# Turning more attention weights by VectorE and DRAM, normalising in the gate, one shared stretch of SBUF, and a planner with backward passes

## The chip, the cores and the metric

The kernel runs on one core of one Trainium2 chip. The metric is the device time of one execution in microseconds (us). A measurement runs the kernel several times and takes the median; a profiled execution gives the trace from which all rows come. Engines are named as the profile names them: PE (TensorE matmul), PEld (TensorE weight load), DVE (VectorE), ACT (ScalarE), POOL (GpSimd) and SP (SyncE, which here issues every DMA).

## The reference

One layer of a hybrid encoder on 1024 prompt rows and 32 sample rows of width 1024, all in float32:

```python
hn = rmsnorm(h, g_pre)
qa, ka, va, ga, qb, kb, vb, gb = split(hn @ w_in)      # 8 x 512 columns, 8 heads of 64 each side
# A: band attention with a clipped relative bias; a frame sees its chunk of 64 and 8 chunks before it
sA = qa @ ka.T * 64 ** -0.5 + bias[rel]
oa = softmax(where(band, sA, -1e30)) @ va
# B: stick-breaking attention, strictly causal
z = qb @ kb.T * 64 ** -0.5
log_1m = where(causal, log_sigmoid(-z), 0)
ob = where(causal, exp(log_sigmoid(z) + reverse_cumsum(log_1m) - log_1m), 0) @ vb
y = concat(oa * silu(ga), ob * silu(gb)) @ w_out
h = h + rmsnorm(y, g_post)
h = h + sigmoid(h @ w_ple_gate) * (p @ w_ple)
```

The keys and values are outputs too. The sample rows attend to a cache of 512 rows as well.

## The kernel before, in words

**Precision.** Every float32 product is done with operands split into a high part and a remainder (`...h` and `...l`, type fp32r), in two or three matmuls.

**Recording and planning.** The body does not emit instructions. A `Recorder` stores each operation with its operands; all get the line of one helper in the profile (L515), so tiles must be told apart by name. `order()` then walks through a model of the engines, with a planner's cost for each operation (`cost`), a start and a margin for each DMA (`DMA_START`, `DMA_MARGIN`), and picks for each engine the ready operation of the lowest key. A key is the place at which the operation was recorded, shifted by the hand-kept tables `AHEAD_OF` and `AHEAD_AT`. The result is a fixed order on every queue. DMAs all stand in SP's queue.

**Stages.** First come norms, transposes of `x` (`ptx`) and a part of the product with `w_ple` (`ple`). Then eight attention stages, pairs of heads in the order A0, B0, A1, B1, ... A3, B3. Each pair p has two heads. While a pair's attention runs, `weave` mixes in the projections of the next pair (`col_steps`, tiles `mm_kA` and so on, 72 matmuls of 352 columns for each output of 128 columns), so that PE has other work between the steps of attention. The last stage holds the gate projections `gA`, `gB` instead. Last come the output products (`o0P` to `o3P`) and the gate products (`g0P` to `g3P`).

**One head of attention** is `attention(ab, p, h)`. It goes over eight query tiles i of 128 rows. `scores(i)` multiplies the queries `L` with `kd` and `kl` into PSUM (`SA`, `SB`). For A, DVE adds the bias and takes the running minimum of the negated scores into `om`, ACT takes the exponential into `be` with the row sum in `statA`, DVE takes the reciprocal and POOL scales `be` by it. For B two sigmoids, a scan and a product on POOL do the same job. A's tile i sees the blocks i-4 to i, so tiles 4 to 7 have five blocks of 128 keys.

`weights_t(i)` turns the weights, keys onto partitions, and splits them into `wTh` (ACT) and `wTl` (DVE). It does this in one of two ways. Either PE transposes each 128x128 block into PSUM (`ptwA`, `ptwB`), four blocks to a bank. Or, for the tiles in `ROUND`, DVE transposes 32x32 squares (`om<-be`), one DMA writes the result to DRAM (`swapA`, `swapB`), and four DMAs read it back in place (`be<-swapA`). `ROUND` names tile 5 for A and tiles 4, 5 and 6 for B.

`values(g)` multiplies the turned weights of four query tiles with the values into `PVA` or `PVB`; g is 0 for tiles 0 to 3 and 1 for tiles 4 to 7. For g = 1 of A, its first matmul reads a block that all four tiles see, so it needs tile 7's weights at once. Tiles are turned `LAG_T` = 2 units behind their scores, and values follow behind that.

**Buffers.** The attention weights lie in two rings, `Arena` "om" (3076 columns) and "be" (3640), which are granted in recording order; turned weights lie in two more rings.

**The gate** (`mms` in `col_steps`, kind "g") loads the head pair's output `og` from `o_dr`, computes acc * sigmoid(acc) and multiplies it by `og` on POOL.

Of the kernel before, what the change touches and what calls it, by code (L numbers as in the profile page):

```python
# [13 lines left out]
P = 128  # L14
# [14 lines left out]
    ('ACT', 'L'): 329, ('ACT', 'S'): -1196, ('ACT', 'be'): -16, ('ACT', 'kd'): 796,  # L29
    ('ACT', 'newh'): -56, ('ACT', 'oT'): -600, ('ACT', 'om'): -36, ('ACT', 'p'): -23,  # L30
    ('ACT', 'v'): 51, ('DVE', 'Kl'): 1140, ('DVE', 'Vh'): -16, ('DVE', 'gT'): -158,
    ('DVE', 'om'): -178, ('DVE', 'ot'): 166, ('DVE', 'uu'): -34, ('DVE', 'vt'): 131,
    ('DVE', 'wl'): 758, ('DVE', 'wls'): 131, ('POOL', 'kl'): 934, ('POOL', 'wl'): 27,
    ('SP', 'GP'): 272, ('SP', 'Kcs'): -461, ('SP', 'be'): 17, ('SP', 'o'): 49,
    ('SP', 'pp'): -611, ('SP', 'stv'): -823,
}
AHEAD_AT = {
    (0, 'ACT', 'sq'): -249, (0, 'DVE', 'pleo'): -309, (1, 'ACT', 'stv'): 1111, (1, 'DVE', 'stat'): -309,
    (1, 'PE', 'ptw'): 174, (2, 'ACT', 'be'): 54, (2, 'ACT', 'v'): 127, (2, 'ACT', 'wTh'): -885,
    (2, 'ACT', 'wh'): -57, (2, 'DVE', 'S'): -238, (2, 'DVE', 'ot'): -112, (2, 'DVE', 'vx'): -293,  # L40
    (3, 'ACT', 'Kh'): -162, (3, 'ACT', 'be'): 443, (3, 'ACT', 'ot'): -574, (3, 'ACT', 'stq'): 399,
    (3, 'ACT', 'w'): 692, (3, 'ACT', 'wTh'): -1352, (3, 'DVE', 'Kcs'): -84, (3, 'DVE', 'S'): -1167,
    (3, 'DVE', 'Vh'): 222, (3, 'DVE', 'w'): -332, (3, 'PE', 'PV'): 1076, (3, 'PE', 'Ss'): 1432,
    (3, 'SP', 'kd'): -118, (3, 'SP', 'kl'): -63, (4, 'ACT', 'be'): 76, (4, 'ACT', 'om'): 38,
    (4, 'DVE', 'S'): -1067, (4, 'DVE', 'vt'): -1007, (4, 'DVE', 'wTl'): 571, (5, 'ACT', 'stq'): -509,
    (5, 'ACT', 'wh'): 1431, (5, 'DVE', 'stat'): 886, (5, 'DVE', 'vt'): -279, (5, 'POOL', 'om'): -449,
    (6, 'ACT', 'be'): 27, (6, 'ACT', 'v'): 29, (6, 'ACT', 'wTh'): 103, (6, 'DVE', 'om'): 123,
    (6, 'DVE', 'ot'): 37, (6, 'POOL', 'ksS'): 600, (6, 'POOL', 'om'): 364, (6, 'SP', 'be'): 463,
    (7, 'ACT', 'newh'): 1036, (7, 'ACT', 'wTh'): -428, (7, 'DVE', 'L'): -198, (7, 'DVE', 'S'): 1202,
    (7, 'DVE', 'Vl'): -1133, (7, 'DVE', 'kt'): 76, (7, 'DVE', 'om'): 204, (7, 'DVE', 'w'): -825,  # L50
    (7, 'DVE', 'wTl'): -310, (7, 'PE', 'ptw'): 1440, (7, 'SP', 'bias'): -214, (7, 'SP', 'o'): 69,
    (7, 'SP', 'swap'): -328, (8, 'ACT', 'sgg'): -941, (8, 'DVE', 'S'): -79, (8, 'DVE', 'Vl'): 272,
    (8, 'DVE', 'om'): 183, (8, 'DVE', 'sgg'): -911, (8, 'POOL', 'sgg'): 256, (8, 'SP', 'Kcs'): 610,
# [8 lines left out]
ROUND = {"A": ((5,),), "B": ((4,), (5,), (6,))}  # L62
LAG_T = 2
LAG_V = 2
SPACE_S = {'A': 0.15, 'B': 0.05}
SPACE_T = {'A': 0.35, 'B': 0.4}
SPACE_V = {'A': 0, 'B': 0}
PARTS = 4
BEHIND = 2
RATES = (1.0, 0.84, 0.92, 0.94, 1.0, 0.88, 1.14, 1.0)  # L70
# [135 lines left out]
class Op:  # L206
    __slots__ = ("pieces", "eng", "what", "args", "kw", "key", "busy", "late", "ready", "left", "after", "at", "size", "shared", "table")
# [9 lines left out]
DVE_SET, POOL_SET = 137, 110  # L217


class Pool:  # L220
# [8 lines left out]
    def tile(self, shape, dtype, tag=None, name=None, bufs=1):  # L229
        b = Buf(shape, dtype, self, tag or name, name, bufs)  # L230
        line = self.tags.setdefault(b.tag, [])
        b.room = b.tag if bufs == 1 else f"{b.tag}.{len(line) % bufs}"
        after = {line[-1].place} if line else {self.opened} if self.opened else set()
        b.place = self.rec.node("CTL", b.take, (), {}, after)
        if len(line) >= bufs:
            self.rec.turns.append((b.place, line[len(line) - bufs]))
        self.ops.append(b.place)
        line.append(b)
        return b
# [47 lines left out]

class Engine:
# [9 lines left out]
class Recorder:  # L298


    def __init__(self):
        self.with_table, self.old_table, self.stage = [], [], 0
# [32 lines left out]
    def node(self, eng, what, args, kw, after):  # L335
# [3 lines left out]
        o.shared, o.table = False, None  # L339
# [3 lines left out]
    def add(self, eng, what, args, kw):  # L343
# [31 lines left out]
        n = o.key[2]  # L375
        o.key = o.key[0], n + AHEAD_OF.get(kind, 0) + AHEAD_AT.get((self.stage, *kind), 0), n
# [17 lines left out]
    def cost(eng, method, args, kw, writes, reads):  # L394
# [18 lines left out]
        if eng == "POOL":  # L413
            if method == "tensor_tensor":
                if n == 1:
                    return 400, 0
                return 200 + (1.9 if out.buf.dtype == F32 else 2.3) * n, 0
# [10 lines left out]
    def order(self):  # L428

        import heapq  # L430
        for place, old in self.turns:
            place.after.update(x[0] for x in old.uses)
        users = {id(o): [] for o in self.ops}
        for o in self.ops:
            o.left, o.ready = len(o.after), 0.0
            for a in o.after:
                users[id(a)].append(o)
# [3 lines left out]
        now = {e: [] for e in names}  # L441
        for o in self.ops:
            if not o.left:
                heapq.heappush(soon[o.eng], (0.0, o.key, id(o), o))
        out, port, line, table, away, flying = [], 0.0, 0.0, AF.Exp, [], 0
        while len(out) < len(self.ops):
# [11 lines left out]
            while soon[e] and soon[e][0][0] <= t:  # L458
                _, key, n, o = heapq.heappop(soon[e])
                heapq.heappush(now[e], (key, n, o))  # L460
            o = heapq.heappop(now[e])[2]
            if o.shared and e == "DVE" and port > t + DVE_SET:
                held = [x for x in now[e] if not x[2].shared]
                if held:
                    heapq.heappush(now[e], (o.key, id(o), o))
# [3 lines left out]
                    o = pick[2]  # L469
            o.at = t  # L470
            if e == "CTL":
                done = t
            elif e == "SP":
# [4 lines left out]
                o.at = t  # L478
# [5 lines left out]
            else:  # L484
# [6 lines left out]
                done = t + o.busy + o.late  # L491
            out.append(o)
            for u in users[id(o)]:
# [4 lines left out]
                u.ready = max(u.ready, r)  # L498
                u.left -= 1
                if not u.left:  # L500
                    heapq.heappush(soon[u.eng], (u.ready, u.key, id(u), u))
        return out

# [17 lines left out]
def stream_step(  # L521
# [26 lines left out]
    r_dr = scratch([8, 768], "r_dr")  # L548
    vs_dr = {ab: scratch([4, P, NS], f"vs_dr{ab}") for ab in "AB"}
    ple_dr = scratch([T, D], "ple_dr")  # L550

# [27 lines left out]
    ring0, ring1 = Arena(rec, at, "om", 3076), Arena(rec, at, "be", 3640)  # L579
# [50 lines left out]
    def load_x(t):  # L630
# [3 lines left out]
        xt = x34[0][:, (t - 3) * D:(t - 2) * D] if 3 <= t < 7 else ring0.tile([P, D], f"x{t}")  # L634
# [9 lines left out]
    def scale_x(t, xt, n, gp):  # L644
        sq = ring1.tile([P, D], f"sq{t}")
# [44 lines left out]
    def bias_rows():  # L690

        rb = ring0.tile([8, 257], "rb")
        dma(rb, rel_bias[0])
        nc.vector.tensor_scalar(rb, rb, -1.0, None, ALU.mult)
        R = ring1.tile([8, 768], "R")
# [49 lines left out]
    def prep_v(nm, h, tok):  # L745
        r, o = halves(h)
        v2 = opnd[h].tile([P, 8, P], F32R, tag=f"v2{h}", name=f"v2{nm}{h}")
        nc.scalar.copy(v2[:, :, r], tok[:, 0:8, r])
        nc.vector.tensor_tensor(v2[:, :, o], tok[:, 0:8, r], f(v2[:, :, r]), ALU.subtract)
# [17 lines left out]
    def keys_out(ab, p, src, o_p, o_s):  # L767
# [4 lines left out]
        def turn():  # L772
            out = at2.tile([P, NT, P], F32, tag="tok", name=f"kt{ab}{p}", bufs=2)
            x = out.rearrange("p b c -> p (b c)")[:, 0:n + NS]
# [9 lines left out]
    def values_out(ab, p, src, o_p, o_s, then):  # L784
# [5 lines left out]
        def turn():  # L790
# [8 lines left out]
            out = at2.tile([P, NT, P], F32, tag="tok", name=f"vt{ab}{p}", bufs=2)  # L799
            box["out"] = out  # L800
            nc.vector.transpose(out[:, 8, 0:NS], st[:, SEQ:T])

        def back():
            out = box["out"]
            nc.scalar.copy(out[:, 0:8, :].rearrange("p b (g f) -> p g b f", g=4), src()[:, 0:SEQ].rearrange("p (g b f) -> p g b f", g=4, f=32))
            later(o_p[0, 0, :, h2, :].rearrange("(b p) h d -> p b (h d)", p=P), out[:, b0:8, :])
            sample_rows(o_s[0, 0, :, h2, :].rearrange("p h d -> p (h d)"), out[:, 8, 0:NS])
            then(out)
# [9 lines left out]
    def col_steps(j):  # L818
# [53 lines left out]
        def after_v(tok):  # L872
            src_of["v", ab, p] = tok
            dma(vs_dr[ab][p], tok[:, 8, 0:NS])
# [11 lines left out]
    def attention(ab, p, h):  # L886
# [22 lines left out]
        def rooms(i):  # L909
# [3 lines left out]
            if g not in whole:  # L913
                n = sum(cost(x) for x in g) * P
                whole[g] = ring0.tile([P, n + more * len(g)], f"om{nm}_{i}"), ring1.tile([P, n], f"be{nm}_{i}")
# [5 lines left out]
        def scores(i):  # L921
# [27 lines left out]
            else:  # L949
# [1035 lines left out]
```

## Time and profile before

| | us |
|---|---|
| median of 3 runs | 776.59 (775.98 to 778.51) |
| profiled execution | 776.69 |
| its span, from the first to the last instruction | 774.8 |
| PE busy / DVE busy / ACT busy / POOL busy | 764.6 / 600.0 / 526.7 / 473.1 |
| mean granted TensorE clock | 0.999 |

The span is 1.9 us shorter than the execution's time. A row of groups reads: line, engine, operation, out<-in with partitions x elements, count | busy time in us, mean ns of one | idle time of the engine before them and what ended it. In the timeline a row is start, length, engine, operation and how many of them in a row.

### The profile page before, as it was taken

What the parts mean: (1) busy time and instruction counts of PE and PEld (TensorE: products, weight loads), DVE (VectorE), ACT (ScalarE), POOL (GpSimd) and SP (SyncE); (2) the same over time, 40 slices, a digit from 0 to 9 for tenths busy, and PEclk for the clock granted to TensorE, in tenths of its full rate; (3) what the DMA queues carried; (4) which work ended last, traced back from release to release, by engine and by line L of the source; (5) the groups of instructions that cost most, each with busy time, mean ns of one, the idle gap of its engine ahead of it and who ended that gap; (6) DMA issues with size and microseconds to landing.
All of it is one profiled execution on the core that took longest, in us unless ns stands there. A gap on an engine that the chain in (4) does not pass through costs nothing.

```text
span 774.8 us, 14446 instructions
## 1 busy us (share of the span) xinstructions
PE 764.6 (99%) x4486; PEld 706.7 (91%) x4486; DVE 600.0 (77%) x1127; ACT 526.7 (68%) x1138; POOL 473.1 (61%) x551
## 2 busy tenths in 40 slices
PE   8999999999999999999999999999999999999997
PEld 6999999999999999999999899999998887888786
DVE  6827768788788899777788788778554687998975
ACT  5646775886687777796767786665447878775561
POOL 5626535463686556766877587665652539798533
PEclk9999999999999999999999999999999999999999
DMA  9736645656868748757958877877689957869644
GB/s 298 247 117 183 155 98 163 154 157 179 219 178 236 190 135 254 198 158 237 229 191 223 237 226 207 245 191 221 180 280 297 302 166 227 260 203 343 231 160 136
DMA packets 190303, 161.00 MB, mean 208 GB/s; under 512 B 65346, under 2 KB 155242, under 8 KB 190227
## 3 DMA queue, kind: packets, MB, share of 16 engines
q1 hardware_dynamic: 190226, 160.08, 70.1%
q8 instruction: 36, 0.59, 0.3%
q14 instruction: 41, 0.33, 0.1%
HBM read 98.12 MB, written 53.50 MB: 196 GB/s over the span
## 4 chain that ended last, share of the span: by engine, by line
PE 89%; POOL 3%; DVE 3%; DMA 2%; ACT 1%; issue 1%; SPq 1%; POOLq 0%; ACTq 0%; DVEq 0%
PE mm_vB L515 6%; PE mm_gB L515 6%; PE mm_gA L515 6%; PE mm_qB L515 6%; PE mm_vA L515 5%; PE mm_kB L515 5%; PE mm_kA L515 5%; PE mm_qA L515 4%; PE PVB L515 4%; PE SB L515 4%; PE PVA L515 4%; PE SA L515 4%; PE ptwA L515 3%; PE o3P L515 3%; PE o1P L515 3%; PE g1P L515 3%
## 5 line engine op out<-in xcount | busy, mean ns | idle before, releaser
L515 POOL TENSOR_TENSOR be<-be,om 128x256 f32<-128x256 f32 (+8 forms) x66 | 82.7, 1258 | 72.6 <-DVE om L515 32.0
L515 DVE TENSOR_TENSOR_SCAN om<-om,SB 128x384 f32<-128x384 f32 (+5 forms) x96 | 91.9, 966 | 15.7 <-ACT be L515 8.7
L515 POOL TENSOR_SCALAR be<-be,statA 128x640 f32<-128x640 f32 (+4 forms) x64 | 46.9, 742 | 35.5 <-DVE statA L515 31.7
L515 ACT ACTIVATE om<-SB 128x384 f32<-128x384 f32 (+5 forms) x96 | 46.0, 495 | 20.3 <-DVE SB L515 16.1
L515 ACT ACTIVATE be<-SB 128x384 f32<-128x384 f32 (+5 forms) x96 | 44.7, 497 | 7.8 <-DVE om L515 4.1
L515 ACT ACTIVATE be<-om,statA 128x640 f32<-128x640 f32 (+4 forms) x64 | 44.4, 695 | 6.2 <-DVE statA L515 4.0
L515 DVE TENSOR_TENSOR wTl<-ptwA,wTh 128x512 fp32r<-128x512 f32 (+2 forms) x80 | 37.0, 480 | 12.5 <-ACT wTh L515 11.8
L515 ACT CAST wTh<-ptwA 128x512 fp32r<-128x512 f32 (+2 forms) x80 | 31.8, 427 | 18.2 <-PE ptwA L515 17.6
L515 DVE TENSOR_TENSOR wTl<-be,wTh 128x640 fp32r<-128x640 f32 (+2 forms) x32 | 35.7, 1123 | 6.0 <-ACT wTh L515 5.3
L515 PE MATMUL ptwA<-ident,be 128*128 128x128 f32 x200 | 32.3, 273 | 0.9 <-POOL qsS L515 0.9
L515 PE MATMUL SB<-kdB,LB 128*128 128x384 f32 (+5 forms) x96 | 33.1, 349 | 0.0
L515 PE MATMUL SB<-klB,LB 128*128 128x384 f32 (+5 forms) x96 | 32.7, 345 | 0.0
L515 DVE CUSTOM_DVE_ANT_0 om<-SA,biasA 128x320 f32<-128x320 f32 (+3 forms) x64 | 30.1, 482 | 2.5 <-PE SA L515 2.2
L515 PE MATMUL SA<-kdA,LA 128*128 128x320 f32 (+2 forms) x96 | 30.8, 324 | 0.4 <-DVE statsA L515 0.3
L515 DVE STREAM_TRANSPOSE om<-be 128x640 f32<-128x640 f32 (+2 forms) x32 | 29.8, 932 | 1.1 <-POOL be L515 0.9
L515 PE MATMUL SA<-klA,LA 128*128 128x320 f32 (+2 forms) x96 | 29.6, 314 | 0.0
L515 DVE TENSOR_TENSOR wTl<-ptwB,wTh 128x512 fp32r<-128x512 f32 (+3 forms) x48 | 25.4, 545 | 4.9 <-PE PVB L515 2.4
L515 ACT CAST wTh<-be 128x640 fp32r<-128x640 f32 (+2 forms) x32 | 25.6, 809 | 5.0 <-DMA be<-swapB 4.6
L515 POOL TENSOR_TENSOR klA<-stkA,kdA 64x1024 fp32r<-64x1024 f32 (+2 forms) x9 | 20.0, 2222 | 13.4 <-ACT kdA L515 13.2
L515 ACT CAST wTh<-ptwB 128x512 fp32r<-128x512 f32 (+3 forms) x48 | 22.1, 485 | 8.6 <-PE ptwB L515 5.8
L515 POOL TENSOR_TENSOR gB<-gB,gB 128x256 f32<-128x256 f32 x32 | 26.5, 846 | 2.2 <-DMA kdB<-kdB 1.6
L515 PEld LDWEIGHTS ptwA<-ident,be 128*128 128x128 f32 x200 | 24.8, 140 | 2.6 <-POOL qsS L515 1.2
(696 smaller groups left out, 2653.1 us busy)
## 6 DMA issues: line engine op xcount, KB each, us to landing
oB<-in_w_out_dram SPq DMA_DIRECT2D x16, 256.0 KB, 3.6
sum_dro<-oB SPq DMA_DIRECT2D x16, 256.0 KB, 2.8
gB<-in_w_ple_gate_dram SPq DMA_DIRECT2D x16, 256.0 KB, 4.3
sum_drg<-gB SPq DMA_DIRECT2D x16, 256.0 KB, 2.6
x<-in_x_prompt_dram SPq DMA_DIRECT2D x16, 256.0 KB, 4.0
h_dr<-h SPq DMA_DIRECT2D x8, 512.0 KB, 3.5
ht<-h_dr SPq DMA_DIRECT2D x8, 512.0 KB, 5.7
raw<-sum_drg SPq DMA_DIRECT2D x16, 256.0 KB, 2.9
```

The source lines that it names most:

```text
L515: getattr(getattr(tc.nc, o.what[0]), o.what[1])(*args, **kw)
```

## The change

1. `ROUND["A"]` names tiles 5, 6 and 7, each by itself: tiles 6 and 7 of all eight A heads are turned by DVE and DRAM too.
2. A's weights are no longer scaled on POOL. The row sums of a head's eight tiles are collected in one tile `rsum`; after tile 7 one reciprocal of eight columns is taken and stored with one DMA to `over_dr`, query by query. In the stage of the A gates each head pair loads it spread over 64 partitions a head (`over`, [128, 1056]), and POOL multiplies `og` by it before the gate product.
3. The two rings become one `Heap` of 6880 columns. A tile's place is chosen when its turn comes in the plan, from the low or the high end, among what is free then.
4. `order()` first simulates forward, then three times goes backward from the end (`latest`) to give each operation a due time and simulates forward again; engines other than PE pick by due time. Buffers with several copies are given out in the simulation as they come free. The tables `AHEAD_OF` and `AHEAD_AT` have other numbers, as have `SPACE_*`, `RATES`, `SUMS_STEP` and the planner's cost of a POOL product.
5. Smaller: the first 512 rows of `p` are read with four rows to a partition, and the product for them is kept in `ple_early` in that order; the second half of `w_ple` is asked for ahead of `x`; value matmuls are chained in order on PE.

The core of the diff:

```diff
-ROUND = {"A": ((5,),), "B": ((4,), (5,), (6,))}
+ROUND = {"A": ((5,), (6,), (7,)), "B": ((4,), (5,), (6,))}
...
-    ring0, ring1 = Arena(rec, at, "om", 3076), Arena(rec, at, "be", 3640)
+    heap = Heap(rec, at, "be", 6880)
...
 # scores(i), A
-                nc.scalar.activation(w1[:, 0:n], w0[:, 0:n], AF.Exp, bias=m[:, last:last + 1], scale=-1.0, accum_out=m[:, 3:4])
-                nc.vector.reciprocal(m[:, 3:4], m[:, 3:4])
-                nc.gpsimd.tensor_scalar(w1[:, 0:n], w1[:, 0:n], m[:, 3:4], 1.0, ALU.mult, ALU.mult)
+                if i == 0:
+                    box["sums"] = small.tile([P, 8], F32, tag="rsum", name=f"rsum{nm}", bufs=3)
+                r = box["sums"]
+                nc.scalar.activation(w1[:, 0:n], w0[:, 0:n], AF.Exp, bias=m[:, last:last + 1], scale=-1.0, accum_out=r[:, i:i + 1])
+                if i == 7:
+                    was, rec.low = rec.low, 1
+                    nc.vector.reciprocal(r, r)
+                    dma(over_dr[p][h].rearrange("(t q) -> q t", q=P), r)
+                    rec.ops[-1].pieces = SEQ
+                    rec.low = was
...
 # mms(c, part)
+                    if kind == "gA":
+                        over = box["over"] = at2.tile([P, T], F32, tag="stg", name=f"over{p}", bufs=3)
+                        nc.gpsimd.memset(over[:, SEQ:T], 1.0)
+                        for h in range(2):
+                            src = over_dr[p].real[h:h + 1, :].to_broadcast([HD, SEQ])
+                            dma(over[h * HD:(h + 1) * HD, 0:SEQ], Raw(over_dr[p], src))
...
+                if kind == "gA":
+                    nc.gpsimd.tensor_tensor(box["og"], box["og"], box["over"][:, cs], ALU.mult)
                 nc.scalar.activation(sg, acc, AF.Sigmoid)
                 nc.vector.tensor_tensor(sg, acc, sg, ALU.mult)
                 nc.gpsimd.tensor_tensor(sg, sg, box["og"], ALU.mult)
...
 # values(g)
+                if n:
+                    rec.ops[-1].after.add(rec.ops[-2])
...
 # order()
+        out, end = self.simulate(lambda o: o.key)
+        for n in range(PASSES):
+            self.latest(end)
+            last = n == PASSES - 1
+            out, end = self.simulate(lambda o: (o.key[0], o.index + last * o.shift, o.index) if o.eng == "PE" and not PE_LATEST else (0, o.due + last * 10 * o.shift, o.index))
+        return out
...
 # Ple.load_p, Ple.pieces
-                src = src.rearrange("(b p) c -> p b c", p=P)
+                src = src.rearrange("(p b) c -> p b c", b=4)
...
-                args = ... ((ple_dr[t0:t0 + n, :], self.outs[t]),)
+                args = ... ((ple_early[:, t, :], self.outs[t]),)
...
 # Gate
-            dma(self.pl[0:n], ple_dr[self.rows, cols])
+            dma(self.pl[0:n], ple_early[32 * t:32 * t + 32].rearrange("q b c -> (q b) c")[:, cols] if t < 4 else ple_dr[self.rows, cols])
```

More of the change, by code (lines that the diff above doesn't have):

```diff
@@ L50 @@
[L50 to L53, printed above, removed]
[4 rows of a table removed]
+    (0, 'ACT', 'hnh'): 112, (0, 'ACT', 'pleo'): 281, (0, 'ACT', 'sq'): 40, (0, 'PE', 'mm'): 90,
+    (0, 'PE', 'ple'): -100, (0, 'PE', 'ptx'): 186, (0, 'POOL', 'ksS'): -120, (0, 'POOL', 'wh'): 345,
[3 rows of a table added]
@@ new lines @@
+    (7, 'SP', 'o'): -652, (7, 'SP', 'over'): -1276, (7, 'SP', 'sum'): -231, (7, 'SP', 'swap'): -309,
+    (7, 'SP', 'vs'): -390, (7, 'SP', 'wr'): -1346, (8, 'ACT', 'om'): 70, (8, 'ACT', 'sgg'): 1347,
+    (8, 'ACT', 'wTh'): -225, (8, 'DVE', 'S'): 400, (8, 'DVE', 'om'): -477, (8, 'DVE', 'sgg'): -1368,
+    (8, 'PE', 'mm'): 50, (8, 'POOL', 'be'): 1286, (8, 'POOL', 'ogg'): -1147, (8, 'POOL', 'sgg'): -517,
+    (8, 'SP', 'Kcs'): 132, (8, 'SP', 'o'): 1036, (8, 'SP', 'og'): -1299, (8, 'SP', 'over'): 287,
@@ L206 @@
 class Op:
-    __slots__ = ("pieces", "eng", "what", "args", "kw", "key", "busy", "late", "ready", "left", "after", "at", "size", "shared", "table")
+    __slots__ = ("pieces", "eng", "what", "args", "kw", "key", "busy", "late", "ready", "left", "after", "at", "size", "shared", "table", "start", "shift", "due", "size_", "index", "users", "tiles", "old")
 LAND = {"PE": 165, "ACT": 0, "DVE": 0, "POOL": 0, "SP": 0, "CTL": 0}
@@ L491, in order @@
                 done = t + o.busy + o.late
+                last = max(last, free[e])
+            if e != "CTL":
+                o.at, o.start = t, free[e] - o.busy
             out.append(o)
-            for u in users[id(o)]:
+            for u in o.users:
                 if u.eng == e and e != "SP":
@@ L497, in order @@
                     r = done + (0 if u.eng == "CTL" else SEM + (MARGIN if u.eng == "PE" else 0))
[L498 to L502, printed above, removed]
+                come(u, r)
+            for b in o.tiles:
+                b.gone = max(b.gone, done)
+                b.left -= 1
+                if not b.left:
+                    leave(b)
+        return out, last
     def emit(self, tc):
```

318 lines of the change are left out of this document (246 added, 72 removed), and 18 rows, old and new, of tables (AHEAD_AT, AHEAD_OF).

## The prediction

> **What bounds the kernel now.** I read the page first, then the windows, then the timeline around the transposes, the groups and the DMA view.
>
> ```profile
> span 774.8 us, 14446 instructions
> PE 764.6 (99%) x4486; PEld 706.7 (91%) x4486; DVE 600.0 (77%) x1127; ACT 526.7 (68%) x1138; POOL 473.1 (61%) x551
> PE 89%; POOL 3%; DVE 3%; DMA 2%; ACT 1%; issue 1%; SPq 1%; POOLq 0%; ACTq 0%; DVEq 0%
> ```
>
> PE is busy for 764.6 of 774.8 us and carries 89% of the chain that ended last. No other engine passes 77%. But a mean hides stages, so the windows come next (columns: stretch, its length, then busy time of PE, PEld, DVE, ACT and POOL with counts, granted clock, DMA share, GB/s).
>
> ```profile
> 0.00:40.00 40.00, 36.57 (x208) 32.36 (x209) 29.98 (x48) 24.84 (x49) 23.78 (x45) 1.00 0.83 274
> 200.00:280.00 80.00, 80.00 (x525) 77.58 (x524) 68.72 (x144) 60.54 (x144) 52.25 (x69) 1.00 0.67 188
> 280.00:360.00 80.00, 79.95 (x516) 77.52 (x515) 66.76 (x150) 61.25 (x136) 54.14 (x64) 1.00 0.75 212
> 360.00:440.00 80.00, 78.57 (x494) 75.38 (x493) 64.83 (x123) 57.31 (x126) 59.31 (x70) 1.00 0.80 217
> 440.00:520.00 80.00, 79.67 (x505) 76.40 (x504) 65.54 (x131) 55.84 (x127) 54.28 (x61) 1.00 0.78 223
> 520.00:600.00 80.00, 80.00 (x478) 75.90 (x477) 49.59 (x82) 41.66 (x87) 41.90 (x41) 1.00 0.79 243
> 680.00:720.00 40.00, 40.00 (x175) 32.52 (x174) 34.78 (x55) 27.19 (x57) 33.90 (x35) 1.00 0.83 282
> 760.00:775.00 15.00, 9.88 (x55) 8.38 (x53) 8.38 (x15) 2.62 (x6) 5.15 (x4) 0.95 0.49 160
> ```
>
> PE lacks 3.43 us at the start and about 5 at the end. The attention stretches lack only 0.05, 1.43 and 0.33 us, together 1.81. The clock is full there. So PE is the bound wherever the change acts: PE work taken out there shortens the run one for one, as long as nothing else falls behind.
>
> **What leaves PE.** In each of A's eight heads tiles 6 and 7 have five blocks each that PE turned; they now take tile 5's path. In the built programs the count of these transposes falls from 200 to 120, and nothing else on PE changes in number. The price must be a pitch, not a duration, because matmuls overlap.
>
> ```profile
> 201.78 0.48 PE L515 MATMUL mm_qB<-hnl,wh_qB 128*128 128x352 f32 x2
> 202.10 0.60 PE L515 MATMUL ptwA<-ident,be 128*128 128x128 f32 x4
> 202.45 0.41 PE L515 MATMUL mm_qB<-hnl,wh_qB 128*128 128x352 f32 x1
> 202.69 0.32 PE L515 MATMUL mm_qB<-hnh,wh_qB 128*128 128x352 f32 x1
> ...
> L515 PE MATMUL ptwA<-ident,be 128*128 128x128 f32 x200 | 32.3, 273 | 0.9 <-POOL qsS L515 0.9
> L515 PEld LDWEIGHTS ptwA<-ident,be 128*128 128x128 f32 x200 | 24.8, 140 | 2.6 <-POOL qsS L515 1.2 <-issue 0.3
> ...
> 557.15 29.31 PE mm_gB L515 x181
> ```
>
> The last row is a piece of the chain: 181 matmuls of 352 columns in 29.31 us, 0.162 us each; the first row's two start 0.32 us before the next, the same. From 202.10 to 202.69 stand four transposes and one such matmul in 0.59 us. That leaves (0.59 - 0.16) / 4 = 0.1075 us per transpose, and 80 x 0.1075 = **8.6 us** leaves PE. Bounds: by columns alone, 0.162 x 128/352 = 0.059 each, 4.7 us; by the busy time that the group covers, 32.3/200 = 0.161 each, 12.9 us. The weight loads say 24.8/200 = 0.124, 9.9 us. I take 0.1075, because it is a start-to-start time.
>
> The same row gives one transpose a mean of 273 ns. The Trainium skill ("TensorE: Matmul & The Clock Gate", Part 4: PE-mode transpose) states about 275 ns for a 128x128 transpose in a kernel's context. The trace agrees on that as a duration; as a price it would make the sum 22 us (an estimate from the page), and the four rows above, where four pass in 0.43 us, speak against it.
>
> **What the other engines get.** For 16 tiles (two in each of eight heads) the copy and the subtraction from PSUM, one of 512 and one of 128 columns, become one VectorE transpose, one cast and one subtraction of 640 columns from SBUF.
>
> ```profile
> L515 DVE STREAM_TRANSPOSE om<-be 128x640 f32<-128x640 f32 x16 | 13.3, 832 | 0.3 <-POOL be L515 0.2
> L515 DVE TENSOR_TENSOR wTl<-be,wTh 128x640 fp32r<-128x640 f32 x16 | 17.2, 1075 | 2.5 <-ACT wTh L515 2.0 <-DMA kdA<-kdA 0.3
> L515 DVE TENSOR_TENSOR wTl<-ptwA,wTh 128x512 fp32r<-128x512 f32 x32 | 21.5, 679 | 9.3 <-ACT wTh L515 9.0
> L515 DVE TENSOR_TENSOR wTl<-ptwA,wTh 128x128 fp32r<-128x128 f32 x32 | 8.9, 279 | 1.4 <-ACT wTh L515 1.2
> L515 DVE RECIPROCAL statA<-statA 128x1 f32<-128x1 f32 x64 | 9.2, 155 | 6.1 <-ACT be L515 5.6
> L515 ACT CAST wTh<-be 128x640 fp32r<-128x640 f32 x16 | 11.7, 729 | 0.4 <-PE PVB L515 0.4
> L515 ACT CAST wTh<-ptwA 128x512 fp32r<-128x512 f32 x32 | 18.7, 588 | 10.7 <-PE ptwA L515 10.4
> L515 ACT CAST wTh<-ptwA 128x128 fp32r<-128x128 f32 x32 | 8.6, 267 | 2.8 <-PE ptwA L515 2.5
> L515 POOL TENSOR_SCALAR be<-be,statA 128x640 f32<-128x640 f32 (+4 forms) x64 | 46.9, 742 | 35.5 <-DVE statA L515 31.7
> L515 POOL TENSOR_TENSOR sggA<-sggA,oggA 128x352 f32<-128x352 f32 x12 | 13.7, 1146 | 4.2 <-DMA oggA<-o_dr 2.5 <-DVE sggA L515 1.7
> ```
>
> DVE: 16 x (0.832 + 1.075 - 0.679 - 0.279) = +15.2; 64 reciprocals of 0.155 become 8, -8.7; net **+6.5 us** on 600. ACT: 16 x (0.729 - 0.588 - 0.267) = **-2.0**. POOL: the 64 scalings go (-46.9); 12 products `over` x `og` of the size of the last row come (+13.8); net **-33 us** on 473. All three stay under 80%, and nothing of this lies on PE's path by its amount. POOL's new products stand in the gate stretch, where POOL has 25.7 us free in 440:520 and 38.1 in 520:600. Behind each of them on POOL wait the last B heads' products, which feed PE; the cost there lies between 0 and, if all 13.8 us delayed PE, 13.8; I take 0, nearest to the free time in those rows.
>
> ```profile
> q1 hardware_dynamic: 190226, 160.08, 70.1%
> ...
> swapA<-om SPq DMA_DIRECT2D x8, 320.0 KB, 3.5
> be<-swapA SPq DMA_DIRECT2D x32, 80.0 KB, 2.5
> ```
>
> DMA: 16 tiles write and read 320 KB each, 10.5 MB; eight loads of `over`, 256 KB each, 2.1 MB. That is 12.6 on 160.08 MB, so the share rises from 70.1% to about 76%. In 520:600 and 680:720 the share is 0.79 and 0.83 with PE without a gap, so I take 0. New are eight stores of 1024 single numbers. No row has one; from above, at the mean packet (0.701 x 16 x 774.8 / 190226 = 46 ns) 64 packets on each of 16 engines take 2.9 us, all engines; from below, 0. Their reader is a gate in the last attention stage: 0 on the path. The Trainium skill ("DMA: Bandwidth & Descriptors", Specifications) counts below 512 B as slow, read-modify-write; by it the stores would sit at the upper bound, off the path all the same, and no run here shows one.
>
> SP issues 96 more DMAs than its 880. They hold what is queued behind them only while they wait, above all the four reads behind the landing of their write.
>
> **The wait that is added.** PE's first value matmul of a head's upper half needs tile 7's turned weights. They now come by a round trip. One of tile 5, as it is now:
>
> ```profile
> 317.60 0.84 DVE L515 STREAM_TRANSPOSE om<-be 128x640 f32<-128x640 f32 x1
> ...
> 318.47 0.34 SPq L515 DMA_DIRECT2D swapA<-om  x1
> ...
> 323.98 1.85 SPq L515 DMA_DIRECT2D be<-swapA  x4
> ...
> 330.81 0.72 ACT L515 CAST wTh<-be 128x640 fp32r<-128x640 f32 x1
> ...
> 332.02 0.81 DVE L515 TENSOR_TENSOR wTl<-be,wTh 128x640 fp32r<-128x640 f32 x1
> ...
> L515 DVE CUSTOM_DVE_ANT_0 om<-SA,biasA,statA 128x320 f32<-128x320 f32 x32 | 17.6, 549 | 3.9 <-PE SA L515 0.5 <-PE PVA L515 0.5 <-DVE statA L515 0.3
> L515 ACT ACTIVATE be<-om,statA 128x640 f32<-128x640 f32 x32 | 26.5, 830 | 2.1 <-DVE Vl2sA L515 1.1 <-DVE statA L515 0.6 <-DVE Kl1sA L515 0.2
> ```
>
> It takes 15.2 us, of which 0.84 + 3.5 + 1.85 + 2.5 + 0.72 + 0.81 = 10.2 are work and the rest is queueing. Ahead of it stand the minimum (2 x 0.549) and the exponential (0.83), 1.9 us; the scaling on POOL (0.742) that stood there is gone. So tile 7 needs about 17.1 us as things run now, 12.1 at best. What covers it is other PE work: in the changed program 132 to 174 matmuls stand on PE between tile 7's last score matmul and that first value matmul. At 80.00 us / 525 = 0.152 us each (window 200:280) that is 20.1 to 26.5 us. The tightest head (A, pair 2, second head) has 3 us to spare, the others more. Tile 5 now has 150 to 205 matmuls and B's tile 6 has 133 to 204, and these stretches lose 1.81 us in all. So I take **0** for the new wait, with bounds of -1.8 (the present stalls go) and +8 (1 us in each head).
>
> **Order and memory.** The order of every queue is new, and one shared stretch replaces two rings. There is no row for either; between 0 and the 1.81 us of middle stalls can be gained. At the start the first `x` tile is issued earlier:
>
> ```profile
> 12.88 0.66 PE L515 MATMUL ptx<-ident,be 128*128 128x128 f32 x4 [1.22 <-DVE be L515]
> 438.19 0.30 PE L515 MATMUL ptwA<-ident,be 128*128 128x128 f32 x1 [0.90 <-POOL qsS L515]
> ```
>
> The 1.22 us may go, or come again behind the weights that now load later: -1.2 to +1.2, taken as 0. The second row is half of the middle's lost time, and it is a transpose waiting for its operand, of which fewer remain. `p` in another layout and `ple_early` change no count that PE sees; PE's warm-up covers their start.
>
> **Sum.** The profiled execution took 776.69 us for a span of 774.8, and the median is 776.59. 776.6 - 8.6 = **768.0 us**. About 0.3% (2.3 us) is what a measurement here can tell from no change: faster is under 774.3, slower over 778.9.
>
> **Rivals.** (a) More goes than the transposes: the better order also removes the 1.81 us and the 1.22. For it: the 0.90 us row. Against it: the new round trips are waits of the same kind. 768.0 - 3.0 = 765.0 us; down to 763.5 if the transposes cost as much as their weight loads (9.9). (b) Part is eaten: tile 7's weights, or a buffer of the shared stretch, come 0.6 us late in each of 8 heads: +4.8, 772.8 us. (c) Slower: the round trip decides. SP serves DMAs in order, so one read waiting for its write's landing holds the next head's transfers. From 8.6/8 = 1.1 us lateness per head the gain is gone; at 1.6 us it is 776.6 - 8.6 + 12.8 = 780.8. For that the trip in the tightest head must take over 4 us longer than the 15.2 shown. Against it: B's three trips per head run today without a gap in 200:280. (d) A transpose holds PE for its whole 273 ns: 80 x 0.273 = 21.8, 754.8 us. Against it: the pitch rows. (e) Nothing changes, since the tiles are still turned on PE: the count 120 excludes it.
>
> **Chances.** Forecast (766 to 771) 0.52, (a) 0.24, (b) 0.10, (c) 0.11, (d) 0.03. Of (b) some 0.06 lies under 774.3 and 0.04 above; of (c) 0.02 falls within 0.3%. So faster 0.85, same 0.06, slower 0.09. The range 763.5 to 775 leaves out (c), (d) and a tail of (b).
>
> **What would show it.** Right: PE's transposes of A's weights at x120; PE busy near 756 us; the middle windows losing no more than 2 us; the POOL group of 64 scalings gone. Wrong: gaps before `PVA` released by ACT or DVE (`wTh`, `wTl`), released in turn by `be<-swapA`, of 1 us or more in each A head; or POOL waiting for `over` in the gate stretch with PE gaps behind it.

## The result: 829.4 us, slower by 6.7%

| | before | after |
|---|---|---|
| median of 4 runs each, us | 776.29 (775.96 to 778.51) | 829.38 (825.74 to 830.33) |
| ratio | | 1.0669, 95% interval 1.0630 to 1.0707 |
| profiled execution, us | 776.69 | 829.82 |
| its span, us | 774.8 | 827.6 |

Times are medians of undisturbed runs: one run of all that follow, 793.1 us of the version e14, lies over 1.5% above the fastest of its kernel and is left out.

The page of the changed kernel: span, busy time of the engines, PE and PE's granted clock in 40 slices, the DMA queue with its share, and the start of the chain that ended last.

```profile
span 827.6 us, 14287 instructions
PE 772.4 (93%) x4406; PEld 707.4 (85%) x4406; DVE 610.6 (74%) x1071; ACT 527.3 (64%) x1122; POOL 445.7 (54%) x503
PE   9999988999999959999959969979999999999997
PEclk9999999999999989999979988999999999999999
q1 hardware_dynamic: 210450, 172.70, 78.9%
PE 32%; DMA 3%; DVE 1%; ACT 1%; SPq 1%; issue 0%; ACTq 0%; DVEq 0%
```

PE has 80 matmuls less (4406 against 4486) and yet is busy for longer. It now stands idle for 827.6 - 772.4 = 55.2 us, before for 10.2. The 40 slices show it in a few deep notches (5, 5, 6, 7), and the clock falls in or behind the same slices. The chain of waits can be followed back through 38% of the span only and says nothing of the rest. No engine became the bound: DVE, ACT and POOL are all under 75%.

The attention stretches (length, then busy PE, PEld, DVE, ACT, POOL with counts, granted clock, DMA share, GB/s):

```profile
280.00:360.00 80.00, 67.24 (x418) 64.36 (x417) 57.31 (x120) 49.85 (x105) 40.00 (x45) 0.96 0.91 203
360.00:440.00 80.00, 66.81 (x392) 63.31 (x391) 53.84 (x84) 50.11 (x107) 48.80 (x56) 0.94 0.87 200
440.00:520.00 80.00, 71.65 (x435) 68.13 (x434) 59.85 (x130) 49.93 (x115) 37.12 (x50) 0.94 0.85 206
520.00:600.00 80.00, 73.76 (x452) 71.03 (x451) 55.89 (x85) 41.03 (x91) 56.38 (x62) 0.98 0.88 219
```

These four lose 12.76 + 13.19 + 8.35 + 6.24 = 40.5 us; before they lost 1.8. What PE waited for (us in total, times, longest):

```profile
PE SB L731 <- DVE be L731: 11.1, 5, 6.7
PE SA L731 <- DMA klA<-klA: 5.8, 1, 5.8
PE PVsA L731 <- DVE otA L731: 5.2, 1, 5.2
PE SsB L731 <- ACT QhsB L731: 4.6, 1, 4.6
PE PVA L731 <- ACT wTh L731: 4.6, 5, 1.6
```

The sign that the forecast had named, gaps before `PVA` behind `wTh`, is there with 4.6 us, in five waits and so not in each of the eight heads. Most of the loss stands elsewhere: single waits of 4 to 7 us, before B's scores, before A's keys, before the sample heads. Work that has nothing to do with the turned tiles is late. So something that they share is likely to be late.

**One such place.** These are 2-us windows around two of the eight stores of row sums, and below them rows of the timeline.

```profile
278.00:280.00 2.00, 2.00 (x15) 1.91 (x13) 2.00 (x7) 1.29 (x4) 1.68 (x2) 1.00 0.90 272
280.00:282.00 2.00, 2.00 (x15) 1.98 (x14) 1.36 (x4) 1.13 (x4) 1.86 (x4) 1.00 0.45 58
282.00:284.00 2.00, 2.00 (x18) 1.98 (x17) 1.97 (x4) 1.79 (x5) 0.99 (x5) 1.00 2.70 133
284.00:286.00 2.00, 2.00 (x13) 1.89 (x13) 2.00 (x4) 0.66 (x2) 0.94 (x1) 1.00 0.44 6
286.00:288.00 2.00, 2.00 (x14) 1.99 (x13) 1.58 (x3) 0.54 (x1) 0.60 (x1) 1.00 0.48 6
288.00:290.00 2.00, 1.57 (x12) 1.27 (x10) 0.00 (x0) 0.00 (x0) 0.00 (x0) 1.00 0.52 17
290.00:292.00 2.00, 0.00 (x0) 0.00 (x0) 0.00 (x0) 0.00 (x0) 0.00 (x0) 1.00 0.86 131
292.00:294.00 2.00, 0.00 (x0) 0.00 (x0) 0.00 (x0) 0.00 (x0) 0.00 (x0) 0.90 1.67 121
294.00:296.00 2.00, 0.00 (x0) 0.00 (x0) 0.84 (x1) 1.47 (x3) 0.00 (x0) 0.50 1.21 22
296.00:298.00 2.00, 1.70 (x5) 1.51 (x6) 1.96 (x4) 0.87 (x1) 0.00 (x0) 0.50 0.74 50
298.00:300.00 2.00, 2.00 (x10) 2.00 (x9) 0.81 (x2) 1.94 (x4) 0.00 (x0) 0.50 0.73 28
```

```profile
280.03 0.42 SPq L731 DMA_DIRECT2D over_dr<-rsumA  x1
281.83 0.53 SPq L731 DMA_DIRECT2D swapB<-be  x1
282.42 0.45 SPq L731 DMA_DIRECT2D over_dr<-rsumA  x1
...
294.05 4.90 SPq L731 DMA_DIRECT2D be<-swapB  x4
294.08 1.47 ACT L731 ACTIVATE be<-SB 128x448 f32<-128x448 f32 x3 [7.33 <-DMA swapB<-be]
...
295.16 2.27 DVE L731 TENSOR_TENSOR_SCAN be<-be,SB 128x448 f32<-128x448 f32 x2 [7.54 <-ACT be L731]
...
296.30 0.80 PE L731 MATMUL SB<-kdB,LB 128*128 128x512 f32 x1 [6.73 <-DVE be L731]
```

Read the last column of the windows. The DMAs move 272 GB/s, then two stores of 4 KB each are issued, and from 284 to 288 the core moves 6 GB/s. The packets that are under way then take so long that their time, booked where they start, makes a share of 2.70. The write of one of B's round trips, issued between the two stores at 281.83, lands only at about 294, some 12 us later. The next in SP's queue are the four reads of that trip, so SP issues nothing either between 285.4 and 294.05. ACT, DVE and PE wait for that write one behind the other, 7.33, 7.54 and 6.73 us. PE's granted clock falls to 0.50 after some 4 us without work, and the first 4 us behind the gap run at half speed as well. The Trainium skill ("TensorE: Matmul & The Clock Gate", Part 1: The HAM clock gate) says that the array falls to half its clock after an idle window of about 3.4 us. The trace agrees within what it resolves: PE ends its work at 289.6 (1.57 us of 288:290), 292:294 has a mean of 0.90, which puts the fall at about 293.6, and 294:296 has 0.50.

The rows that answer to the forecast's own:

```profile
L731 PE MATMUL ptwA<-ident,be 128*128 128x128 f32 x120 | 20.4, 273 | 1.7 <-DVE wTl L731 1.7
L731 DVE STREAM_TRANSPOSE be<-be 128x640 f32<-128x640 f32 x32 | 26.6, 832 | 3.2 <-ACT be L731 2.7 <-POOL be L731 0.3
L731 POOL TENSOR_TENSOR oggA<-oggA,over 128x352 f32<-128x352 f32 x12 | 13.1, 1094 | 10.5 <-DMA oggA<-o_dr 10.5
swapA<-be SPq DMA_DIRECT2D x24, 320.0 KB, 4.3
be<-swapA SPq DMA_DIRECT2D x96, 80.0 KB, 3.1
```

The counts are the forecast's, and the durations nearly so (120 transposes, 0.832 us a turn, 1.09 us a product where 1.15 was taken). The landings grew: 4.3 us for a write (3.5 before) and 3.1 for a read (2.5 before).

### The profile page after: what moved, and what is told of

It is laid out like the page before. It is cut to its first block, busy times and chain, and to the rows that moved or that the text cites. A ratio compares the mean times of both kernels' runs of the same rounds, so it can differ in the third digit from the quotient of the medians.

```text
span 827.6 us, 14287 instructions
## 1 busy us (share of the span) xinstructions
PE 772.4 (93%) x4406; PEld 707.4 (85%) x4406; DVE 610.6 (74%) x1071; ACT 527.3 (64%) x1122; POOL 445.7 (54%) x503
## 3 DMA queue, kind: packets, MB, share of 16 engines
q1 hardware_dynamic: 210450, 172.70, 78.9%
## 5 line engine op out<-in xcount | busy, mean ns | idle before, releaser
L731 DVE TENSOR_TENSOR_SCAN be<-be,SB 128x384 f32<-128x384 f32 (+5 forms) x96 | 92.1, 967 | 38.9 <-ACT be L731 28.7
L731 POOL TENSOR_TENSOR be<-be 128x128 f32<-128x128 f32 (+8 forms) x66 | 83.9, 1277 | 66.8 <-DVE be L731 29.7
L731 ACT ACTIVATE be<-SB 128x384 f32<-128x384 f32 (+5 forms) x192 | 84.8, 496 | 45.2 <-DMA swapB<-be 14.9
L731 ACT ACTIVATE be<-be,statA 128x640 f32<-128x640 f32 (+3 forms) x64 | 44.6, 697 | 17.1 <-DVE statA L731 10.1
L731 DVE STREAM_TRANSPOSE be<-be 128x640 f32<-128x640 f32 (+3 forms) x56 | 48.4, 868 | 8.1 <-POOL be L731 5.2
L731 POOL TENSOR_TENSOR oB<-oB,oB 128x256 f32<-128x256 f32 x32 | 23.9, 765 | 38.6 <-DMA oB<-in_w_out_dram 31.6
L731 DVE CUSTOM_DVE_ANT_0 be<-SA,biasA 128x320 f32<-128x320 f32 (+2 forms) x64 | 30.1, 480 | 5.5 <-PE SA L731 3.2
L731 DVE TENSOR_TENSOR wTl<-ptwA,wTh 128x128 fp32r<-128x128 f32 (+3 forms) x48 | 22.4, 482 | 8.2 <-ACT wTh L731 6.0
L731 POOL TENSOR_TENSOR klB<-stkB,kdB 64x1024 fp32r<-64x1024 f32 x8 | 19.9, 2489 | 9.8 <-ACT kdB L731 4.1
L731 PE MATMUL ptwB<-ident,be 128*128 128x128 f32 x144 | 22.4, 281 | 2.4 <-POOL be L731 2.4
```

What stands on the lines that cost most here:

```text
L731: getattr(getattr(tc.nc, o.what[0]), o.what[1])(*args, **kw)
```

## The experiments

**Theory A:** a store of 1024 separate 4-byte numbers to neighbouring places in DRAM holds up every DMA of the core for several us. **Rival B:** the 16 added round trips, the higher DMA share or the new order cost the time. In all experiments but those named otherwise the order on PE, DVE, ACT and POOL is the one of the kernel that they start from.

### The same stores in runs of 32 bytes

```diff
-    dma(over_dr[p][h].rearrange("(t q) -> q t", q=P), r)
+    dma(over_dr[p][h].rearrange("(q t) -> q t", q=P), r)
```

> The changed kernel with one thing different: each store of the row sums writes 128 runs of 32 bytes instead of 1024 single numbers of 4 bytes (the 1024 numbers lie in another order, so 1/sum goes to other queries; the order on every engine is the same). Theory A (the 1024 writes of 4 bytes hold up every DMA of the core for some 9 us, eight times): the time falls from 829 to 765-778. Rival B (the 16 added round trips, the higher DMA share or the new plan cost the time): it stays over 815. In the trace A expects DVE's, ACT's and PE's stalls at the eight stores to go.

Measured: **780.49 us** (778.73 to 782.78, 10 runs), 1.0041 of before, interval 1.0027 to 1.0056. 48.9 of the 53.1 us are gone with one change of layout; the time is 2.5 us above the range that theory A had named. The page, and the windows around the same two stores (now at 272.5 and 274.9):

```profile
span 778.4 us, 14287 instructions
PE 760.6 (98%) x4406; PEld 699.6 (90%) x4406; DVE 613.3 (79%) x1071; ACT 528.3 (68%) x1122; POOL 450.7 (58%) x503
...
272.00:274.00 2.00, 2.00 (x15) 1.91 (x15) 1.58 (x5) 0.45 (x2) 1.86 (x4) 1.00 0.44 137
274.00:276.00 2.00, 2.00 (x16) 1.98 (x15) 1.79 (x4) 1.79 (x6) 1.24 (x4) 1.00 0.62 200
276.00:278.00 2.00, 2.00 (x16) 1.97 (x15) 1.97 (x4) 1.34 (x3) 0.70 (x4) 1.00 0.70 203
```

No hold-up is left: 137 to 203 GB/s and no gap on PE. PE's idle time falls from 55.2 to 778.4 - 760.6 = 17.8 us, and its busy time by 11.8 us, with a mean clock of 0.998 where it was 0.981. B as the main cause is out. (In this kernel and those built on it, up to the complete versions below, 1/sum goes to other queries.)

### How the price goes with the size and place of the writes

```diff
 # runs of 8 bytes
+    dma(over_dr[p][h].rearrange("(u q v) -> q u v", q=P, v=2), r.rearrange("q (u v) -> q u v", v=2))
 # 32-byte runs, and behind them a second store that nobody reads, 64 bytes apart
+    far = far_dr[p].real[h].rearrange("(t q s) -> q t s", q=P, s=16)[:, :, 0]
 # the same, 8 bytes apart, neighbours from one partition
+    far = far_dr[p].real[h].rearrange("(q t s) -> q t s", q=P, s=2)[:, :, 0]
```

> The changed kernel with each store of the row sums as 512 runs of 8 bytes (same order on every engine, numbers in another order). If the hold-up goes by the number of writes (A), each lasts some 4.5 us instead of 9, and buffers cover more of it: 778-800. If any run far under 512 bytes costs the same (A2): 825-832, and the kernel with 32-byte runs too. If only the 4-byte size is slow (A3): 765-778.

> The changed kernel with two DMAs in the place of each store: the 128 runs of 32 bytes into the place that is read later, and behind it the 1024 single numbers into a scratch area, each 64 bytes from the next, which nobody reads. Same order on the engines. If each small write has its price wherever it goes (A): 820-835, as after. If the writes wait for one another because neighbours share a piece of memory (A4): 765-780. Rival B: over 815 either way; it is told apart by the kernel with 32-byte runs alone.

> As the kernel with the second store spread by 64 bytes (784.0 us), but the 1024 single numbers of that store stand 8 bytes apart, and the eight neighbours in 64 bytes come from one partition. If writes collide because different DMA engines write into the same 64 bytes (A4a): 781-787. If neighbouring writes wait for one another whichever engine sends them (A4b): 800-835.

| store, for each of 8 heads | separate writes in 64 bytes | us | over 780.5 |
|---|---|---|---|
| 128 runs of 32 bytes | 2 | 780.49 | |
| the same, and 1024 numbers 64 bytes apart | 1 | 783.98 (783.86 to 784.66) | +3.5 |
| 512 runs of 8 bytes | 8 | 794.84 (792.76 to 796.03) | +14.3 |
| runs of 32, and 1024 numbers 8 bytes apart | 8 | 806.40 (803.68 to 810.46) | +25.9 |
| 1024 numbers, adjacent (the change) | 16 | 829.38 | +48.9 |

The 8-byte runs and the 8-byte spacing fell into ranges named beforehand; the 64-byte spacing came out 4 us above its own. So it is neither the number of writes alone (1024 of them 64 bytes apart cost 3.5 us in all eight stores together) nor the small size alone. It is many separate writes into the same small piece of memory. With eight of them in 64 bytes, 512 cost 14.3 and 1024 cost 25.9, so there the number counts as well. That they come from different partitions doesn't make it: the 8-byte spacing has its neighbours from one partition and still costs 25.9. How large the piece is, and where in the memory path the writes wait, was not tried. The forecast cited the Trainium skill ("DMA: Bandwidth & Descriptors", Specifications: read-modify-write below 512 bytes). Runs of 32 bytes are far below that and hold up nothing in the windows above, so that threshold is not what sets the price here.

### The stores alone, in the kernel before

```diff
+    dma(over_dr[p][h].rearrange("(t q) -> q t", q=P), ident[:, 0:8])   # one per A head, never read
```

Once with nothing to wait for, so that all eight are issued together early on, and once behind the first output store of each A head.

> The kernel before with nothing of the change but eight extra stores: after tile 7 of each A head 1024 single numbers (from the identity matrix) go to a scratch area in DRAM that nobody reads. The order on all engines stays, SP has eight DMAs more. Theory A: the stores alone cost 35-60 us: 812-836. Rival B (the plan, the round trips): 776-780.

> The kernel before with eight extra stores of 1024 single numbers (identity matrix into a scratch area that nobody reads), each issued on SP right behind the first store of an A head's output, so that they are spread over the attention stages and not sent in one bunch. The order of all engines stays. If a store holds up all DMAs for some 9 us wherever it stands and little covers it: 805-830. If the order of before has more room behind its loads than the changed kernel's: 782-800. If only a bunch hurts: 776-780.

Measured: **801.89 us** in one bunch (1.0314, 1.0289 to 1.0339) and **842.07 us** spread (1.0864, 1.0822 to 1.0907). Both lie outside the ranges of theory A, the bunch 10 us below and the spread stores 12 us above. In the bunch, SP's queue, then DMA traffic with the stores, then the same stretch of the kernel before:

```profile
24.50 20.76 SPq L515 DMA_DIRECT2D over_dr<-ident  x8
```

```profile
27.00:51.00 24.00, 23.53 (x151) 22.24 (x149) 10.81 (x20) 8.67 (x20) 7.03 (x9) 1.00 1.40 2
```

```profile
27.00:51.00 24.00, 24.00 (x156) 23.00 (x155) 14.97 (x25) 11.44 (x24) 8.42 (x12) 1.00 0.58 190
```

For 24 us the core moves 2 GB/s where it moved 190: 3.0 us a store. SP's eight issues take 20.76 us. PE then loses one gap of 20.8 us. Spread out, the stores hurt more. The window below begins 3.4 us behind the issue of one of them (208.61), and the rows are what PE waited for in the whole run:

```profile
212.00:219.00 7.00, 2.05 (x15) 1.79 (x13) 0.00 (x0) 0.00 (x0) 4.08 (x10) 0.88 0.73 28
```

```profile
PE PVA L515 <- ACT wTh L515: 25.8, 6, 6.7
PE SsA L515 <- ACT QhsA L515: 10.2, 2, 5.8
```

Behind one store among other transfers the traffic stays at 28 GB/s for 7 us. SP takes 7.98 us there for three reads of a round trip, and gaps take the clock down: over the whole run its mean is 0.969, and PE's busy time grows from 764.6 to 784.3 us.

None of the change's other parts is in these two kernels, so the stores alone are enough for a loss of 24 to 65 us.

### What is left: 780.5 against 768.0

```diff
 # without the DMAs of the round trips of A's tiles 6 and 7
+    if ab == "A" and i > 5: rec.ops[-1].what = lambda *a: None
 # tiles 6 and 7 back on PE, all else of the change kept
-ROUND = {"A": ((5,), (6,), (7,)), "B": ((4,), (5,), (6,))}
+ROUND = {"A": ((5,),), "B": ((4,), (5,), (6,))}
```

> The kernel with stores of 32-byte runs (780.5 us), without the DMAs of the 16 added round trips: tiles 6 and 7 of A are neither written to DRAM nor read back (their weights stay half turned), all else in the same order on every engine. PE's stalls there were 21.1 us against 8.8 before. If the added trips, their waits or their DMA load, make the 12 us of extra stalls: 766-770, that is 776.6 less the 8.6 of the 80 transposes. If the new plan makes them: 778-782.

> The kernel with stores of 32-byte runs, but tiles 6 and 7 of A turned by PE again, as before; 1/sum in the gate, the shared stretch and the planner stay (the planner makes another order). If the trips make the extra stalls, the 80 transposes (+8.6) and the lost stalls (-12) give 775-779. If the planner and the shared stretch make them: 785-792.

Measured: **776.94 us** without the trips (772.64 to 777.60, 10 runs; 0.9984 of before, 0.9966 to 1.0002), and **783.36** with the tiles back on PE (780.89 to 783.49; 1.0062, 1.0039 to 1.0085). Both lie between the two ranges named beforehand, so neither cause has it all. The trips' DMAs cost 780.5 - 776.9 = 3.6 us. The rest, 776.9 - 768.0 = 8.9, stays without them. With the old PE work and the old number of trips, planner, shared stretch, gate product and the small parts of the change together are still 783.4 - 777.7 = 5.7 us slower than the kernel before beside them. So a loss of this size doesn't need the turned tiles; how much of it is the order alone is not shown, since that kernel runs in another order again. By span less busy time, PE is idle for 17.8 us in the 780.5-us kernel, 15.9 without the trips and 10.2 before. (Before ran at 776.3 to 778.5 us beside the different sets of runs, so these terms are good to about 1 us.) One number of the plan, or one line of the change in the old plan, shows how much can hang on the order:

```diff
-    heap = Heap(rec, at, "be", 6880)
+    heap = Heap(rec, at, "be", 6816)
 # kernel before, one line of the change
-ROUND = {"A": ((5,),), "B": ((4,), (5,), (6,))}
+ROUND = {"A": ((5,), (6,), (7,)), "B": ((4,), (5,), (6,))}
```

> The kernel with stores of 32-byte runs (780.5 us) with one number changed: the shared stretch has 6816 columns instead of 6880. The work is the same, but the planner makes another order. It measures what the order alone is worth. If the order matters little (as my forecast took it): 778-783. If the tables fit one order only and a new one brings new waits: 788-800.

> The kernel before with one line of the change: tiles 5, 6 and 7 of A go by VectorE and DRAM (old planner, old rings, scaling on POOL). My forecast's sum of the transposes alone: 768 (766-771). If the 16 added trips cost what their removal gave back in the changed kernel (3.6 us): 770-773. If any order that the tables were not made for loses some 10 us: 778-795.

Measured: **791.11 us** (790.47 to 793.89) with the smaller stretch, 10.6 more than the same work in the other order and with 64 columns more. **830.34 us** (828.59 to 831.92) for the old planner with the three trips: the forecast's 8.6 us came out as a loss of 53.7 against the 776.67 measured beside it, without any 4-byte store. That is far outside all three ranges named beforehand. Its waits are many (before `SA` 7.1 us, before `SB` 5.6 and 4.5, before `mm_kB` 4.9). ACT waited only 4.8 us for `be<-swapA` to land, so the trips' own landings are a small part. That the tables were made for other work is the likely cause; no run separates it from the added trips.

Two waits of the 780.5-us kernel, in rows. First ACT in front of a value copy. Its four reads were issued from 302.0 to 303.9, and the profile puts the wait down to the DMA issued right behind them; the copy itself reads `stvA`:

```profile
302.00 1.93 SPq L731 DMA_DIRECT2D stvA<-swapA  x4
...
308.44 1.05 ACT L731 COPY vtA<-stvA 128x1024 f32<-128x1024 f32 x1 [2.62 <-DMA sum_dro<-oB]
```

Then one late round trip, from its reads to the value matmul:

```profile
440.94 2.16 SPq L731 DMA_DIRECT2D be<-swapA  x4
...
445.92 0.72 ACT L731 CAST wTh<-be 128x640 fp32r<-128x640 f32 x1 [0.37 <-DMA be<-swapA]
...
446.70 1.29 PE L731 MATMUL PVA<-wTh,v2A 128*128 128x512 f32 x4 [1.84 <-ACT wTh L731]
```

### Versions that compute the whole reference

```diff
 # 32-byte runs; the gate's product reads `over` turned, tile by tile, in 2 or 3 pieces a chunk
+    turned = over[:, 0:SEQ].rearrange("p (q t) -> p t q", t=8)
+    nc.gpsimd.tensor_tensor(og[:, c], og[:, c], turned[:, t, q:q + n], ALU.mult)
 # the same, three instructions moved in the planned order
+    sink(ops, ("ACT", "vtA2", 0), ("ACT", "otB11_1_1", 0))
+    sink(ops, ("ACT", "LA20", 0), ("DVE", "wTlB10_1", -1))
+    sink(ops, ("PE", "PVA30_1", 0), ("PE", "mm_vB3_0", 11))
```

> The changed kernel, complete, in exactly its own order on PE, DVE, ACT and SP: the store writes 128 runs of 32 bytes (query within a tile first), and the gate's product reads `over` through a turned view, in two or three pieces a chunk on POOL (32 POOL products instead of 12, which end in time). If the stores are all that separates 829 from 780: 779-783. If POOL's extra pieces reach PE: 783-788.

> The kernel e14 with three places of the planned order changed by hand, where an engine stood in front of a DMA that had not landed or a longer job: ACT's copy vtA2 behind the four casts and copies that follow it (PE lost 2.5 us there), the cast LA20 behind the turned weights of B10 (1.2 us), the value matmuls PVA30_1 eight matmuls of vB and two tiles of transposes later (2.0 us, where they wait for a round trip). If the remaining 12 us are such waits of the new order, one by one: e14 less 3-6 us, 774-778. If another chain is late right behind each: within 1.5 us of e14.

Measured: **783.98 us** (e14: 780.85 to 788.28), 1.0082 of before, interval 1.0052 to 1.0112; and **786.57** (e15: 780.82 to 789.60), 1.0108, interval 1.0074 to 1.0142. The first is the change with its fault mended: 45 us faster than the change, still 0.8% slower than before. It lies in the range named for POOL's extra pieces reaching PE, but the trace of the second, which has the same pieces, shows no wait of PE in front of the gate projections, so these 3.5 us stay unexplained. The second is no faster: the waits moved. In the 780.5-us kernel PE's gaps are 2.3 us at 309, 0.6 at 328 and 1.8 at 445 us; with the moved instructions they are 1.7 at 309, 1.6 at 327 and 2.7 at 447, the last now before a transpose: 4.7 us in sum before and 6.0 after.

A third way, turning 1/sum on VectorE and storing 32 runs of 128 bytes, was run twice. In the first kernel one staging tile serves all heads and is overwritten by the next head before its store has read it, so some queries get another head's sum; the DMAs are the same. The lines are those of the second kernel.

```diff
+    nc.vector.transpose(sums, sums)                       # 32x32 squares
+    for g in range(4): dma(rows[g], sums[32 * g:32 * g + 8, :])
```

> The changed kernel with 1/sum turned by one VectorE transpose of 32x32 squares before it is stored: 32 runs of 128 bytes a head in four DMAs, in the order that the gate reads. Heap of 6816 columns in place of 6880, and so another order. Theory A: 776-784, near the kernel with 32-byte runs. If anything under 512 bytes were slow: over 800.

> The changed kernel with 1/sum turned on VectorE (one transpose of 32x32 squares in its own tile) and stored as 32 runs of 128 bytes a head, query by query; the stretch has 6808 columns. This computes the whole reference. Theory A: the hold-ups at the stores are gone, and the time is that of the order that the planner makes: 778-798. If stores far under 512 bytes stay slow: over 800.

Measured: **795.40 us** (792.98 to 796.84) and **789.13** (787.45 to 791.53). Both have another stretch and so another order; the first has the stretch of the 791.1-us kernel. The first lies between its two ranges, the second inside that of A. They agree with A and tell nothing finer.

Last, the mended kernel planned with later landings of all DMAs:

```diff
-DMA_START, DMA_DONE, DMA_RATE, DMA_MARGIN = 1950, 300, 320.0, 2000
+DMA_START, DMA_DONE, DMA_RATE, DMA_MARGIN = 1950, 300, 320.0, 3000    # and 4500
```

> The kernel e14 (784 us) with the planner's margin behind each DMA (DMA_MARGIN) at 3000 ns instead of 2000, nothing else: the planner takes DMAs to land later and makes another order. If late DMAs are what its order misses: 772-781. If any other order than the one that the tables were made for loses 10 us, as the 6816-column stretch did: 788-800.

> As the run with 3000 ns, with a margin of 4500 ns. If late DMAs are what the order misses: 770-781, at or below the one with 3000. If any other order loses: 788-805.

Measured: **809.68** (808.96 to 810.53) and **849.01** (847.36 to 851.54). Both are slower than any of the ranges named beforehand. More margin made it worse, so planning with later DMAs is not the cure. The complete versions, nearly the same work in five orders, took 784.0, 786.6, 789.1, 809.7 and 849.0 us. Which waits of a new order cost how much, one by one, stays open. No complete version beat the kernel before.

## Why the prediction was wrong

**The step that failed: the eight stores at "0 on the path".** The forecast looked for the path behind the store's own reader, a gate in the last attention stage. The cost fell on the other DMAs then in flight: B's round trip, A's keys, the next weights. The runs showed 48.9 us for eight stores, 6.1 each. The size was bounded at 0 to 2.9 us of all DMA engines for one store, from packets of other sizes. Eight in a bunch came to 3.0 us each, so that upper end was nearly right, and by luck: no row of the trace of before had a store of single numbers, and what their price hangs on, writes that crowd into a small piece of memory, is not in the bound. Behind one store among other transfers the traffic stayed down for 7 us. That a store stops what others wait for was not among the rivals.

**The second step: order and memory at 0.** The bounds there were what could be gained (0 to 1.81 us) and 1.2 at the start; a loss in the middle was not bounded at all. With the 4-byte stores out, 8.9 us of loss stay when the trips' DMAs go too. That the planner walks through a model, and that its tables are fitted to one list of work, stood in the code; changing both at once should have had a bound on the losing side.

**The transposes** (8.6 us): the count fell to 120 as told, and with the same planner PE's busy time shows the price: 766.8 us with tiles 6 and 7 on PE, 760.6 without them (32-byte runs) and 759.3 (the same without the trips). That puts 80 transposes at 6.2 to 7.5 us, an estimate, since the first kernel runs in another order: inside the bounds of 4.7 to 12.9 and somewhat under 8.6. Against the kernel before, PE's busy time fell by only 4.0 us, from 764.6 to 760.6, where 756 was forecast; with all 200 transposes it is 2.2 us higher under the new planner, and why is open. The 8.9 above is worked out with 8.6 and holds these differences too.

**The added wait** (0, bounds -1.8 to +8): 3.6 us by the run without the trips, inside its bounds. Rival (c) had the right mechanism for it, and by chance 780.8 us, within 0.3 us of the kernel with 32-byte runs; but it was to come from trips alone, at 1.6 us a head, and they cost 0.45.

**The other engines:** DVE +6.5 forecast, +10.6 measured; ACT -2.0 and +0.6; POOL -33 and -27.4; DMA share 76% and 78.9% (77.2% without the hold-ups). Small errors beside 53.1 us. (A slip in the sums: the lower end of rival (a) is 776.6 - 9.9 - 3.0 = 763.7 us, not 763.5.)

Together: 776.6 - 8.6 + 3.6 + 8.9 + 48.9 = 829.4, where 8.9 is what remains after the measured terms.

## What to carry to other kernels

Ask of every new DMA not only who waits for its data, but what else is in flight while it runs: here a store of 4 KB cost 6.1 us, and a round trip of 320 KB each way 3.6 / 16 = 0.2. When numbers have to be turned on their way to DRAM, write what each partition holds as one run and turn on the reading side, where an engine with time to spare can do it through its access pattern (POOL here, with 3.5 us between the 780.5-us kernel and the complete one). A plan fitted to one list of work is part of the kernel's time: before counting a gain of 1%, ask what a new order may lose.

## What the hardware showed that was not expected

Eight stores of 1024 adjacent 4-byte numbers, 32 KB in all, cost 48.9 us in one kernel and 65 in another (842.1 - 776.7); while they are in flight the core's DMA traffic falls from 272 to 6 GB/s, and in a bunch of eight to 2 GB/s for 24 us. Spread 64 bytes apart the same 1024 writes cost 3.5 us for all eight. And a gap on PE costs more than its length: after some 4 us of it the granted clock stood at 0.50, and over the whole kernel the 4-byte stores made 11.8 us of longer busy time beside 37.4 us of idle time.
